# A two-layer decoder trunk on one core: splits of the gated outputs and output weights moved earlier, final norm issued in four pieces

## The chip, the cores and the metric

The kernel runs on one core of a Trainium2 chip, in one launch. The metric is device time in microseconds (us); 1124.77 us is the median of three runs of the kernel before. The engines named below are PE (TensorE, the matmuls), DVE (VectorE), ACT (ScalarE), POOL (GpSimd) and SP (SyncE, which here only issues transfers). Each engine works through its own queue strictly in order, so an instruction that waits holds up everything queued behind it.

## The reference, cut to what matters

Width and sequence length are both 1024, float32 throughout, batch 1, two layers.

```python
# layer 0: gated short convolution;  layer 1: causal differential attention
def diff_attn_mixer(h, w_in, w_out, ...):          # 8 heads, two softmax maps each, V_DIM = 128
    q, k, v, z = jnp.split(h @ w_in, 4, axis=-1)
    ...
    a = p[:, :, 0] - lam * p[:, :, 1]              # difference of two softmaxes
    o = einsum(a, v)                               # per head
    o = rmsnorm(o, subln_g) * (1.0 - lambda_init)  # per-head norm
    return (o * jax.nn.silu(z)) @ w_out            # the gated output y = o * silu(z), then w_out

for i in range(2):
    x = x + mixer_i(rmsnorm(x, norm_g[i]))
return rmsnorm(x, final_g)                         # the final norm
```

## The kernel before

Everything is held transposed: features on the 128 partitions, tokens along the free axis. A 1024 x 1024 operand is eight tiles of 128 features by 1024 tokens. A matmul in full precision is made of three cheaper ones: each operand is split into a high part (rounded to the matmul's format) and a low part (what is left), and `mm3` (line 132) sums high x high, high x low and low x high. So before any operand can be multiplied it must be split: one copy that rounds (`xh`, `wh` or `wo`) and one subtraction (`xl`, `wl`, or the second `wo`). For eight feature tiles and 512 tokens one output takes 24 matmuls.

The attention layer runs as 64 rounds, `step(s)`, head by head and 128 queries at a time, in an order written out by hand; nothing is rescheduled. In each round PE computes scores, DVE finds their maximum, ACT the exponentials, DVE, ACT and POOL the difference of the two maps, and SP issues a transposing transfer of it, which the values product reads three to four rounds later. From round 56 on `opening` and `closing` add work for the output product: weights of the last layer are fetched (`fetch_w`), scaled by the sub-norm's gain and split (`prep_w`: two ACT passes, lines 884 and 885, one subtraction, line 886), and the gated outputs of the heads, stored to memory earlier, are fetched two heads at a time (`fetch_y`) and split (`splits`, `split_y`: ACT line 855, DVE line 856). In the names of the trace these splits are `xh` and `xl` once more, read from `yr`, because they take over the tiles of the layer's input.

After round 63 `tail` computes the outputs of the first 512 tokens. Outputs 0, 2 and 3 are built up as heads become ready, then 1 and 4, then 5, 6 and 7. Head 7 comes last: `last_factors` and the function `rest` it returns spread its norm factors over the partitions with two matmuls (`bps`, line 955), multiply (line 956) and split. `out_take` (a take, line 903) adds the residual on DVE, and has ACT square and scale the sum (lines 910, 915) and POOL add up the squares (line 912). Then come the second 512 tokens in two blocks of 256, eight outputs each, 24 matmuls per output.

`finish` is the final norm of a block, a generator: `next(ending)` issues its next piece. Its pieces are given out between the outputs of the next block: DVE sums up and splits the squares, PE adds them over the partitions (`cps`), POOL takes the root, DVE spreads the result to `dg`, PE broadcasts it (`bps`, line 188), and POOL multiplies and SP stores pair by pair.

Buffers that matter here: the accumulators `mm` are three, used in turn, so an output can start only when the take three outputs earlier has been done; fetched `yr` and `wr` tiles share three slots; the residuals `xr` have two slots each for even and odd outputs.

Of the kernel before, what the change touches and what calls it, by code (L numbers as in the profile page):

```python
# [11 lines left out]
F32 = mybir.dt.float32  # L12
F32R = mybir.dt.float32r
# [4 lines left out]
ALU = mybir.AluOpType  # L18
# [32 lines left out]
def trunk(ctx: ExitStack, tc: tile.TileContext, a: dict, out: bass.AP):  # L51
# [4 lines left out]
    def f(t):  # L56
        return t.bitcast(F32)
# [103 lines left out]
    def norm_cols(sqs, n, rdst, tmp=None):  # L161

        if tmp:
            for sq in sqs[1:]:
                V.tensor_tensor(out=sqs[0], in0=sqs[0], in1=sq, op=ALU.add)
            sqs = bf16_parts(sqs[0], *tmp, (V, V))
        cps = col_sums(sqs, n)
        ms = const.tile([P, KC], F32, tag="ms", bufs=1, name="ms")
        V.tensor_scalar(out=ms[:, :n], in0=cps, scalar1=1.0 / D, scalar2=EPS, op0=ALU.mult, op1=ALU.add)
        G.tensor_tensor(out=rdst, in0=ms[:, :n], in1=neghalf[:, :n], op=ALU.pow)  # L170
# [20 lines left out]
    def norm_rows(rsrc, dst, n, tags, at=None):  # L191

        for b0 in range(0, n, 4):
            nb = min(4, n - b0)
            dgs = sl.tile([P, 2, nb, P], F32R, tag=tags[b0 // 4 % len(tags)], name="dg")
            dgs = dgs[:, 0], dgs[:, 1]
            spread(rsrc[:, b0:b0 + nb], dgs, V)
            bps = rows(dgs, nb, at or ((psm, "mm") if b0 else None))
            if dst is not None:
                A.activation(out=dst[:, b0 * P:(b0 + nb) * P], in_=bps, func=AF.Copy)  # L200
        return bps
# [648 lines left out]

    yh, yl = [], []

    def split_y(h, half, yr):
        s = HALF[half]
        A.activation(out=yh[h][:, s], in_=yr, func=AF.Copy)  # L855
        V.tensor_tensor(out=yl[h][:, s], in0=yr, in1=f(yh[h])[:, s], op=ALU.subtract)  # L856

    raw_y = {}

    def fetch_y(h, half):  # L860

        raw_y[h, half] = yr = r_raw[0].tile([P, 2, 512], F32, name="yr")
        for i in range(2):
            dma(out=yr[:, i, :], in_=yd[h + i, half])

    def splits(h, half):
        yr = raw_y.pop((h, half))
        for i in range(2):
            split_y(h + i, half, yr[:, i, :])

    raw_w = {}

    def fetch_w(d):
        raw_w[d] = r_raw[0].tile([P, D], F32, name="wr")
        dma(out=raw_w[d], in_=a["w_out1"][d])

    def prep_w(d, eng=V):

        wr = raw_w.pop(d)
        if d < 2:  # L880
            wh, wl = (wp.tile([P, D], F32R, tag=t, bufs=2, name=t) for t in ("wh", "wl"))
        else:
            wh, wl = (sl.tile([P, D], F32R, tag=t, name="wo") for t in wtags[d])
        A.activation(out=wr, in_=wr, func=AF.Copy, scale=gsub)
        A.activation(out=wh, in_=wr, func=AF.Copy)
        eng.tensor_tensor(out=wl, in0=wr, in1=f(wh), op=ALU.subtract)
        wo[d] = wh, wl
# [29 lines left out]
    def finish(t0, n, x3s, accs):  # L917

        nb = n // P
        end = t0 + n == S  # L920
        rc = const.tile([P, 4], F32, tag="rc", bufs=2, name="rc")
        tmp = None if end else (sm.tile([P, n], F32, tag="dgl", name="r1"), sm.tile([P, n], BF16, tag="sqw", name="r2"))
        norm_cols(accs, nb, rc[:, :nb], tmp)
        yield
        rt = None if end else r_bc[:, t0:t0 + n]
        rps = norm_rows(rc, rt, nb, r_z.tags[1:])
        yield
        eng, r = (V, rps[:, :n]) if end else (G, rt)
        for d in range(0, KC, 2):
            pair = x3s[d // 2]  # L930
            eng.tensor_tensor(out=pair, in0=pair, in1=r.unsqueeze(1).to_broadcast([P, 2, n]), op=ALU.mult)
            if not end:
                yield
            dma(out=out[d:d + 2, :, t0:t0 + n].rearrange("d p t -> p d t"), in_=pair)
        yield
# [41 lines left out]
    def opening(s):  # L977

        if s == 56:
            q0, q1, q2, q3, spare = (r_q.tags[(r_q.n + 3 + i) % 5] for i in range(5))  # L980
            r_raw.append(Ring(sl, [spare, (wp, "wr0"), (wp, "wr1")]))
            wtags.update({2: r_v.tags[:2], 3: (q0, q1), 5: (q2, q3), 6: r_k.tags[2:]})
            fetch_w(2)
        elif s == 59:
            fetch_w(3)
            fetch_w(0)
        elif s == 61:
            fetch_y(0, 0)
            fetch_y(2, 0)
        elif s == 62:  # L990
            fetch_w(1)
        elif s == 63:
            fetch_y(4, 0)

    def closing(s):

        if s == 56:
            pb = [r_p2.tags[(r_p2.n + i) % 3] for i in (1, 2, 0)]
            wtags.update({4: (r_k.tags[1], pb[0]), 7: (pb[1], pb[2])})
        elif s == 57:  # L1000
            prep_w(2, G)
        elif s == 60:
            prep_w(3, G)
            prep_w(0, G)
        elif s == 61:
            yh[:], yl[:] = new_x()
        elif s == 62:
            splits(0, 0)
        elif s == 63:
            splits(2, 0)  # L1010
            differences(L7, 7)
            for fn in turns:
                fn()
            turns.clear()
            for d in (0, 2, 3):
                pts[d] = psm.tile([P, 512], F32, tag="mm", name="mm")
                part(pts[d], d, 0, 512, (0, 1))
            for t0, n in ((0, 512), (512, 256), (768, 256)):
                order = (0, 2, 3, 1, 4, 5, 6, 7) if not t0 else range(KC)
                wanted.extend((d, t0, n) for d in order)  # L1020

    def tail():
        for d in (0, 2, 3):
            part(pts[d], d, 0, 512, (2, 3))
        head_sums(*last_squares)
        gate_last(0)
        step(NS, False)
        rest = last_factors(0, r_p1.tags[4])
        splits(4, 0)
        split_y(L7 - 1, 0, heads[L7 - 1]["o"][:, HALF[0]])  # L1030
        prep_w(1)
        fetch_w(4)
        fetch_w(5)
        for i in range(3):
            fetch_residual(*wanted.pop(0))
        for d in (0, 2, 3):
            part(pts[d], d, 0, 512, (4, 5, 6))
        pts[1] = pss.tile([P, 512], F32, tag="sc", name="big")
        part(pts[1], 1, 0, 512, range(7))
        step(NS + 1, False)  # L1040
        rest(psa.tile([P, 512], F32, tag="av", name="bps"))
        prep_w(4)
        prep_w(5)
        fetch_w(6)
        fetch_w(7)
        pts[4] = pss.tile([P, 512], F32, tag="sc", name="big")
        part(pts[4], 4, 0, 512, range(7))
        step(NS + 2, False)
        step(NS + 3, False)
        x3a = x3_tiles([r_p1.tags[4], r_p1.tags[0], r_p1.tags[1], r_z.tags[0]], 512)  # L1050
        accs = []
        for d in (0, 2, 3, 1, 4):
            part(pts[d], d, 0, 512, (7,))
            out_take(d, pts[d], 0, 512, x3a, accs)
        fetch_y(0, 1)
        prep_w(6)
        prep_w(7)
        fetch_y(2, 1)
        fetch_y(4, 1)
        pts[5] = psm.tile([P, 512], F32, tag="mm", name="mm")  # L1060
        part(pts[5], 5, 0, 512, range(KC))
        head_sums(*last_squares)
        step(NS + 4, False)
        gate_last(1)
        rest = last_factors(1, r_v.tags[2])
        split_y(L7 - 1, 1, heads[L7 - 1]["o"][:, HALF[1]])
        out_take(5, pts[5], 0, 512, x3a, accs)
        splits(0, 1)
        pt = psm.tile([P, 512], F32, tag="mm", name="mm")
        part(pt, 6, 0, 512, range(KC))  # L1070
        rest(psa.tile([P, 512], F32, tag="av", name="bps"))
        out_take(6, pt, 0, 512, x3a, accs)
        splits(2, 1)
        splits(4, 1)
        pt = psm.tile([P, 512], F32, tag="mm", name="mm")
        part(pt, 7, 0, 512, range(KC))
        out_take(7, pt, 0, 512, x3a, accs)
        ending = finish(0, 512, x3a, accs)
        for t0, tags in ((512, r_v.tags[2:]), (768, r_p1.tags[2:4])):
            x3b = x3_tiles(tags, 256)  # L1080
            accs = []
            for d in range(KC):
                pt = psm.tile([P, 512], F32, tag="mm", name="mm")
                part(pt[:, :256], d, t0, 256, range(KC))
                out_take(d, pt[:, :256], t0, 256, x3b, accs)
                if d:
                    next(ending, None)
            ending = finish(t0, 256, x3b, accs)
        for _ in ending:
            pass  # L1090

# [55 lines left out]
```

## Time and profile before

| what | value |
|---|---|
| median of three runs (lowest, highest) | 1124.77 us (1123.16, 1127.71) |
| the profiled execution, its own time | 1124.44 us |
| its span, first to last instruction | 1122.7 us |
| PE busy | 1062.3 us (95% of the span) |
| DVE, ACT, POOL busy | 595.9, 438.1, 529.9 us |
| mean granted PE clock | 0.967 of full speed |

The profile is of one execution. Its span is 1.7 us shorter than its own device time. All stamps below are microseconds from the start of the span. In a timeline row the first number is the start, the second the time of the merged group, `x3` how many were merged, and the bracket how long the engine stood idle just before and what released it. Busy time of PE is modelled, and a busy PE may still run at half clock.

### The profile page before, as it was taken

Reading aid. Unit: us, or ns where it says so; the run is one execution under the profiler, and the core shown is the slowest. Engines: PE = TensorE matmul, PEld = TensorE weight load, DVE = VectorE, ACT = ScalarE, POOL = GpSimd, SP = SyncE. Lnnn points to the kernel's source line nnn. Section 1 sums busy time; section 2 is a strip of 40 time slices with the busy share of each in tenths; the row PEclk is TensorE's granted clock in tenths of the full one; section 3 lists DMA queues with packets and bytes.
Section 4 is the critical chain, followed back from the end, with each engine's and each line's share of the span. In section 5 each row is a group of like instructions: output and inputs, shape, how many; then the busy total and the mean of one; then the engine's idle time right before and its main releaser. Section 6 shows DMA issues by size and latency. Waiting matters only on the chain.

```text
span 1122.7 us, 15168 instructions
## 1 busy us (share of the span) xinstructions
PE 1062.3 (95%) x5900; PEld 901.2 (80%) x5900; DVE 595.9 (53%) x948; ACT 438.1 (39%) x715; POOL 529.9 (47%) x318
## 2 busy tenths in 40 slices
PE   9899999999999999979979999999999999878896
PEld 6678888888888888868868989888898988656696
DVE  6564133232233322347868686877787687843512
ACT  3211011111111233145746466564656464635322
POOL 7554244244333254345535657383756646412243
PEclk9899999999999999988989999999999999898988
DMA  6221111111111243143474949595656778452132
GB/s 188 76 76 38 57 51 44 57 38 57 40 55 57 100 169 121 67 104 99 101 117 91 173 86 170 95 131 128 140 126 141 132 117 155 108 133 103 51 109 85
DMA packets 123192, 111.86 MB, mean 100 GB/s; under 512 B 88128, under 2 KB 95984, under 8 KB 123120
## 3 DMA queue, kind: packets, MB, share of 16 engines
q1 hardware_dynamic: 123120, 110.90, 42.3%
q8 instruction: 46, 0.75, 0.3%
q14 instruction: 26, 0.21, 0.1%
HBM read 67.82 MB, written 11.59 MB: 71 GB/s over the span
## 4 chain that ended last, share of the span: by engine, by line
PE 77%; DVE 7%; DMA 5%; POOL 5%; ACT 3%; issue 2%; SPq 0%; POOLq 0%; DVEq 0%; ACTq 0%
PE big L132 37%; PE mm L132 25%; PE sc L616 5%; PE mm L525 5%; DMA p<-p 3%; PE av L672 3%; DVE p L639 1%; PE cps L157 1%; POOL p L652 1%; POOL wl L408 1%; DVE nm L621 1%; POOL qt L465 1%; DMA xr<-in_xT 1%; ACT p L644 1%; POOL w3l L254 0%
## 5 line engine op out<-in xcount | busy, mean ns | idle before, releaser
L120 POOL TENSOR_TENSOR wl<-wr,wh 128x1024 fp32r<-128x1024 f32 x37 | 90.1, 2435 | 215.9 <-ACT wh L119 215.9
L132 PE MATMUL mm<-xh,wh 128*128 128x512 f32 (+1 forms) x424 | 163.3, 385 | 4.2 <-ACT xh L855 4.1
L132 PE MATMUL mm<-xl,wh 128*128 128x512 f32 (+1 forms) x424 | 163.8, 386 | 2.9 <-DVE xl L856 2.9
L132 PE MATMUL mm<-xh,wl 128*128 128x512 f32 (+1 forms) x424 | 162.6, 384 | 0.0
L119 ACT ACTIVATE wh<-wr 128x1024 fp32r<-128x1024 f32 x37 | 39.2, 1061 | 294.4 <-PE big L132 293.6
L132 PE MATMUL big<-xh,wh 128*128 128x512 f32 x472 | 146.9, 391 | 2.2 <-DVE cr L289 2.2
L132 PE MATMUL big<-xh,wl 128*128 128x512 f32 x472 | 146.8, 391 | 0.0
L132 PE MATMUL big<-xl,wh 128*128 128x512 f32 x472 | 146.7, 390 | 0.0
L408 POOL TENSOR_TENSOR wl<-wr,wh 128x1024 fp32r<-128x1024 f32 x40 | 95.9, 2398 | 104.2 <-ACT wh L407 99.8
L623 ACT ACTIVATE p<-sc,nm 128x256 f32<-128x256 f32 (+7 forms) x128 | 94.2, 739 | 44.9 <-DVE nm L621 20.8
L132 PEld LDWEIGHTS big<-xh,wh 128*128 128x128 f32 x472 | 88.8, 189 | 20.9 <-issue 2.6
L132 PEld LDWEIGHTS big<-xh,wl 128*128 128x128 f32 x472 | 89.1, 189 | 18.5
L132 PEld LDWEIGHTS big<-xl,wh 128*128 128x128 f32 x472 | 88.9, 188 | 18.6
L132 PEld LDWEIGHTS mm<-xh,wh 128*128 128x128 f32 x424 | 80.2, 189 | 19.9 <-ACT xh L855 5.6
L132 PEld LDWEIGHTS mm<-xl,wh 128*128 128x128 f32 x424 | 80.2, 189 | 18.8 <-DVE xl L856 4.7
L621 DVE TENSOR_REDUCE nm<-sc 128x2 f32<-128x256 f32 (+5 forms) x96 | 91.9, 958 | 3.3
L132 PEld LDWEIGHTS mm<-xh,wl 128*128 128x128 f32 x424 | 80.3, 189 | 15.6
L616 PE MATMUL sc<-kt,qt 128*128 128x512 f32 (+2 forms) x384 | 86.2, 360 | 4.7 <-issue 2.0
L525 PE MATMUL mm<-wh,xh 128*128 128x256 f32 x256 | 74.9, 293 | 1.3 <-DVE tq L460 0.6
L616 PEld LDWEIGHTS sc<-kt,qt 128*128 128x128 f32 x384 | 64.4, 193 | 13.0 <-ACT p L623 3.2
L525 PE MATMUL mm<-wl,xh 128*128 128x256 f32 x256 | 74.5, 291 | 0.0
L525 PE MATMUL mm<-wh,xl 128*128 128x256 f32 x256 | 74.4, 290 | 0.0
(190 smaller groups left out, 2016.5 us busy)
## 6 DMA issues: line engine op xcount, KB each, us to landing
wr<-in_w_in SPq DMA_DIRECT2D x53, 512.0 KB, 3.5
wr<-in_w_out SPq DMA_DIRECT2D x16, 512.0 KB, 4.4
wr<-in_w_v SPq DMA_DIRECT2D x16, 512.0 KB, 3.8
qt<-qt SPq DMA_DIRECT2D x32, 256.0 KB, 3.9
xr<-in_xT SPq DMA_DIRECT2D x15, 512.0 KB, 4.3
x2d<-x SPq DMA_DIRECT2D x8, 512.0 KB, 2.8
kt<-lo SPq DMA_DIRECT2D x32, 128.0 KB, 4.8
rb<-rrd SPq DMA_DIRECT2D x14, 256.0 KB, 4.8
```

The source lines that it names most:

```text
L119: A.activation(out=wh, in_=wr, func=AF.Copy)
L120: G.tensor_tensor(out=wl, in0=wr, in1=f(wh), op=ALU.subtract)
L132: T.matmul(ps[:, o:o + n], lhsT=w[:, s], rhs=r[k][:, t:t + n], start=(k == 0 and r is rh and w is wh), stop=(k == KC - 1 and w is wl))
L157: T.matmul(cps[:, b:b + 1], lhsT=part[:, b * P:(b + 1) * P], rhs=one, start=(i == 0), stop=(i == len(parts) - 1))
L408: G.tensor_tensor(out=self.wl, in0=self.wr, in1=f(self.wh), op=ALU.subtract)
L465: G.tensor_tensor(out=qt[own[m], 1, :], in0=tq[own[m]], in1=f(qt)[own[m], 0, :], op=ALU.subtract)
L525: T.matmul(self.pts[tp][:, i, :], lhsT=x[k][:, ts], rhs=w[:, kk], start=(k == 0 and i == 0 and x is xh and w is wh), stop=(k == KC - 1 and ...
L616: T.matmul(sc[:, i, c0:c1_], lhsT=qt[:, var, ts], rhs=kt[:, c0:c1_], start=(var == 0), stop=(var == 1))
L621: V.tensor_reduce(out=nm[:, ms], in_=sc[:, :, :L], axis=AX, op=ALU.max, negate=True)
L623: A.activation(out=(p1_, p2_)[m][:, :L], in_=sc[:, i, :L], func=AF.Exp, bias=nm[:, m:m + 1], accum_out=st[:, m:m + 1])
L639: V.scalar_tensor_tensor(out=p1_[:, :L], in0=p2_[:, :L], scalar=cs[:, 1:2], in1=p1_[:, :L], op0=ALU.mult, op1=ALU.add)
L672: T.matmul(av[:, qi * P:(qi + 1) * P], lhsT=v[:, kb, es], rhs=at[:, r, :], start=(kb == 0 and r == 0 and v is vh), stop=(kb == qb and v is ...
```

## The change

The diff, whole. `V`, `A`, `G` are DVE, ACT and POOL.

```diff
-    def split_y(h, half, yr):
+    def split_y(h, half, yr, pool=0):
+
         s = HALF[half]
-        A.activation(out=yh[h][:, s], in_=yr, func=AF.Copy)
-        V.tensor_tensor(out=yl[h][:, s], in0=yr, in1=f(yh[h])[:, s], op=ALU.subtract)
+        if pool == 2:
+            G.tensor_copy(out=yh[h][:, s], in_=yr)
+        else:
+            A.activation(out=yh[h][:, s], in_=yr, func=AF.Copy)
+        (G if pool else V).tensor_tensor(out=yl[h][:, s], in0=yr, in1=f(yh[h])[:, s], op=ALU.subtract)
...
-    def splits(h, half):
+    def splits(h, half, pool=(0, 0)):
         yr = raw_y.pop((h, half))
         for i in range(2):
-            split_y(h + i, half, yr[:, i, :])
+            split_y(h + i, half, yr[:, i, :], pool[i])
...
-        tmp = None if end else (sm.tile([P, n], F32, tag="dgl", name="r1"), sm.tile([P, n], BF16, tag="sqw", name="r2"))
-        norm_cols(accs, nb, rc[:, :nb], tmp)
+        if not end:
+            V.tensor_tensor(out=accs[0], in0=accs[0], in1=accs[1], op=ALU.add)
+            accs = bf16_parts(accs[0], sm.tile([P, n], F32, tag="dgl", name="r1"),
+                              sm.tile([P, n], BF16, tag="sqw", name="r2"), (V, V))
+            yield
+        norm_cols(accs, nb, rc[:, :nb])
         yield
         rt = None if end else r_bc[:, t0:t0 + n]
-        rps = norm_rows(rc, rt, nb, r_z.tags[1:])
+        dgs = sl.tile([P, 2, nb, P], F32R, tag=r_z.tags[1], name="dg")
+        dgs = dgs[:, 0], dgs[:, 1]
+        spread(rc[:, :nb], dgs, V)
+        yield
+        rps = rows(dgs, nb)
+        if not end:
+            A.activation(out=rt, in_=rps, func=AF.Copy)
         yield
...
@@ opening
         elif s == 62:
             fetch_w(1)
+            splits(0, 0, (1, 2))
         elif s == 63:
             fetch_y(4, 0)
+            split_y(2, 0, raw_y[2, 0][:, 0, :], 2)
@@ closing
-        elif s == 62:
-            splits(0, 0)
         elif s == 63:
-            splits(2, 0)
+            split_y(3, 0, raw_y.pop((2, 0))[:, 1, :])
@@ tail
         step(NS + 1, False)
+        prep_w(4)
         rest(psa.tile([P, 512], F32, tag="av", name="bps"))
-        prep_w(4)
         prep_w(5)
...
         accs = []
+        prep_w(6)
         for d in (0, 2, 3, 1, 4):
             part(pts[d], d, 0, 512, (7,))
             out_take(d, pts[d], 0, 512, x3a, accs)
+            if d == 3:
+                prep_w(7)
         fetch_y(0, 1)
-        prep_w(6)
-        prep_w(7)
...
         part(pt, 6, 0, 512, range(KC))
-        rest(psa.tile([P, 512], F32, tag="av", name="bps"))
+        splits(2, 1, (2, 0))
         out_take(6, pt, 0, 512, x3a, accs)
-        splits(2, 1)
-        splits(4, 1)
+        splits(4, 1, (0, 2))
         pt = psm.tile([P, 512], F32, tag="mm", name="mm")
         part(pt, 7, 0, 512, range(KC))
+        rest(psa.tile([P, 512], F32, tag="av", name="bps"))
         out_take(7, pt, 0, 512, x3a, accs)
         ending = finish(0, 512, x3a, accs)
+        next(ending)
...
                 if d:
                     next(ending, None)
+            for _ in ending:
+                pass
             ending = finish(t0, 256, x3b, accs)
+            next(ending)
```

The first place is POOL's queue at rounds 61 to 64. `xh` and `xl` are the splits of the gated outputs (of heads 0, 1 and 2 here), `o` the gating of head 6, `p` the low halves of the attention differences of head 7. Before:

```order
L494 TENSOR_TENSOR o<-o,rb 128x512
L494 TENSOR_TENSOR o<-o,th 128x512
L494 TENSOR_TENSOR o<-o,rb 128x512
L494 TENSOR_TENSOR o<-o,th 128x512
L652 TENSOR_TENSOR p_8277<-p_8276,p_8277 128x768
L652 TENSOR_TENSOR p_8358<-p_8357,p_8358 128x896
```

And now:

```order
L494 TENSOR_TENSOR o<-o,rb 128x512
L494 TENSOR_TENSOR o<-o,th 128x512
L860 TENSOR_TENSOR xl_8342<-yr,xh_8334 128x512
L857 CAST xh_8335<-yr 128x512
L860 TENSOR_TENSOR xl_8343<-yr,xh_8335 128x512
L494 TENSOR_TENSOR o<-o,rb 128x512
L494 TENSOR_TENSOR o<-o,th 128x512
L857 CAST xh_8336<-yr 128x512
L860 TENSOR_TENSOR xl_8344<-yr,xh_8336 128x512
L652 TENSOR_TENSOR p_8277<-p_8276,p_8277 128x768
L652 TENSOR_TENSOR p_8362<-p_8361,p_8362 128x896
```

Two rounding copies and three subtractions have come onto POOL, two of the five ahead of the difference's halves; the first rounding copy stays on ACT, a round earlier than it was.

The second place is DVE's queue where the first outputs are taken: `x<-mm,xr` and `x<-big,xr` are the takes of outputs 0, 2, 3 and then 1, 4; `wo<-wr,wo` the last step of splitting a weight. Before:

```order
L886 TENSOR_TENSOR wo<-wr,wo 128x1024 x2
L676 TENSOR_SCALAR o<-av,us 128x256
L903 TENSOR_TENSOR x_8714<-mm,xr 128x512
L903 TENSOR_TENSOR x_8715<-mm,xr 128x512 x2
L903 TENSOR_TENSOR x_8714<-big,xr 128x512
L903 TENSOR_TENSOR x_8716<-big,xr 128x512
L886 TENSOR_TENSOR wo<-wr,wo 128x1024 x2
```

And now:

```order
L890 TENSOR_TENSOR wo<-wr,wo 128x1024
L676 TENSOR_SCALAR o<-av,us 128x256
L890 TENSOR_TENSOR wo<-wr,wo 128x1024
L907 TENSOR_TENSOR x_8714<-mm,xr 128x512
L907 TENSOR_TENSOR x_8715<-mm,xr 128x512 x2
L890 TENSOR_TENSOR wo<-wr,wo 128x1024
L907 TENSOR_TENSOR x_8714<-big,xr 128x512
L907 TENSOR_TENSOR x_8716<-big,xr 128x512
```

The weight of output 6 now stands ahead of the first take, that of output 7 between the takes of outputs 3 and 1.

The third place is DVE's queue at the end of the first 512 tokens. `x<-mm,xr 128x512` is the take of output 7, the ones of 128x256 those of the next block; L165 (now L927), L147 and L148 sum and split the squares. Before:

```order
L903 TENSOR_TENSOR x_8717<-mm,xr 128x512
L903 TENSOR_TENSOR x_8916<-mm,xr 128x256 x2
L165 TENSOR_TENSOR acc<-acc,sq 128x512
L147 TENSOR_TENSOR r_8982<-acc 128x512
L148 TENSOR_TENSOR r_8983<-r_8982 128x512
L169 TENSOR_SCALAR ms<-cps 128x4
L903 TENSOR_TENSOR x_8916<-mm,xr 128x256
```

And now:

```order
L907 TENSOR_TENSOR x_8717<-mm,xr 128x512
L927 TENSOR_TENSOR acc<-acc,sq 128x512
L147 TENSOR_TENSOR r_8918<-acc 128x512
L148 TENSOR_TENSOR r_8919<-r_8918 128x512
L907 TENSOR_TENSOR x_8922<-mm,xr 128x256 x2
L169 TENSOR_SCALAR ms<-cps 128x4
L907 TENSOR_TENSOR x_8922<-mm,xr 128x256
```

The three instructions that sum and split the squares have moved ahead of the takes of the next block's first two outputs.

## Rows read from the trace of the kernel before

**Rows 1.** Waits of PE, 940 to 1123 us; in total, times, longest, us

```profile
PE bps L188 <- DVE dg L180: 5.1, 4, 1.9
```

**Rows 2.** Timeline of PE, start of the splits of heads 2 and 3

```profile
984.55 0.49 PE L132 MATMUL mm<-xh,wh 128*128 128x512 f32 x1 [3.23 <-ACT xh L855]
986.54 0.79 PE L132 MATMUL mm<-xl,wh 128*128 128x512 f32 x1 [1.49 <-DVE xl L856]
```

**Rows 3.** Timeline of DVE, rounds 62 to 64

```profile
974.62 1.29 DVE L856 TENSOR_TENSOR xl<-yr,xh 128x512 fp32r<-128x512 f32 x2 [1.79 <-ACT xh L855]
...
979.92 2.00 DVE L639 SCALAR_TENSOR_TENSOR p<-p,cs,p 128x896 f32<-128x896 f32 x1
984.53 2.56 DVE L856 TENSOR_TENSOR xl<-yr,xh 128x512 fp32r<-128x512 f32 x2 [2.61 <-ACT xh L855]
...
987.51 1.28 DVE L639 SCALAR_TENSOR_TENSOR p<-p,cs,p 128x1024 f32<-128x1024 f32 x1
```

**Rows 4.** Timeline of POOL, the same rounds

```profile
976.72 1.28 POOL L494 TENSOR_TENSOR o<-o,rb 128x512 f32<-128x512 f32 x1 [8.04 <-DVE sc L619]
...
979.32 1.66 POOL L652 TENSOR_TENSOR p<-p,p 128x768 f16<-128x768 f32 x1
984.06 1.88 POOL L652 TENSOR_TENSOR p<-p,p 128x896 f16<-128x896 f32 x1 [3.08 <-ACT p L645]
```

**Rows 5.** Timeline of PE, outputs 4 to 7 and the second half's first

```profile
1011.49 0.80 PE L132 MATMUL big<-xh,wo 128*128 128x512 f32 x1 [3.57 <-ACT wo L885]
...
1019.05 2.69 PE L672 MATMUL av<-p,vt 128*128 128x128 f16 x45
...
1025.08 0.39 PE L132 MATMUL mm<-xh,wo 128*128 128x512 f32 x1
...
1030.53 0.95 PE L157 MATMUL cps<-ones_r,sqo 128*128 128x1 f32 x8
1034.35 0.80 PE L132 MATMUL mm<-xh,wo 128*128 128x512 f32 x1 [2.87 <-ACT wo L885]
...
1043.10 0.64 PE L955 MATMUL bps<-dg,ones_r 128*128 128x512 f32 x2
...
1049.07 0.28 PE L132 MATMUL mm<-xh,wh 128*128 128x256 f32 x1
```

**Rows 6.** Windows: length, busy us of each engine, granted clock, DMA share

```profile
1007.90:1019.05 11.15, 7.54 (x22) 5.34 (x21) 3.83 (x4) 4.82 (x5) 0.00 (x0) 0.69 0.21 71
...
1031.48:1043.10 11.62, 8.72 (x24) 6.46 (x25) 5.92 (x10) 6.28 (x8) 2.86 (x3) 0.71 0.29 102
```

**Rows 7.** Groups by line and shape, 1005 to 1055 us

```profile
L912 POOL TENSOR_TENSOR acc<-acc,sq 128x512 f32<-128x512 f32 x6 | 7.8, 1293 | 41.6 <-ACT sq L910 41.6
...
L886 DVE TENSOR_TENSOR wo<-wr,wo 128x1024 fp32r<-128x1024 f32 x4 | 4.9, 1226 | 10.8 <-ACT wo L885 10.8
L884 ACT ACTIVATE wr<-wr,gsub 128x1024 f32<-128x1024 f32 x4 | 4.5, 1134 | 0.0
L910 ACT ACTIVATE sq<-x 128x512 f32<-128x512 f32 x7 | 4.4, 629 | 10.3 <-DVE x L903 8.3 <-POOL acc L912 2.0
L885 ACT ACTIVATE wo<-wr 128x1024 fp32r<-128x1024 f32 x4 | 4.2, 1056 | 0.1
```

**Rows 8.** Timeline of DVE, takes of the second half's blocks

```profile
1053.86 0.42 DVE L903 TENSOR_TENSOR x<-mm,xr 128x256 f32<-128x256 f32 x1 [0.71 <-PE mm L132]
...
1080.52 0.42 DVE L903 TENSOR_TENSOR x<-mm,xr 128x256 f32<-128x256 f32 x1 [2.46 <-PE mm L132]
1083.40 0.42 DVE L903 TENSOR_TENSOR x<-mm,xr 128x256 f32<-128x256 f32 x1 [2.46 <-PE mm L132]
...
1111.88 0.42 DVE L903 TENSOR_TENSOR x<-mm,xr 128x256 f32<-128x256 f32 x1 [2.46 <-PE mm L132]
```

**Rows 9.** Groups by line and shape, POOL, the whole span

```profile
L379 POOL TENSOR_TENSOR acc<-acc,sq 128x1024 f32<-128x1024 f32 x6 | 18.0, 2999 | 2.0 <-ACT sq L377 2.0
...
L298 POOL TENSOR_SCALAR t<-v,cw 128x1024 f32<-128x1024 f32 x8 | 9.4, 1180 | 0.0
```

## The prediction, on record before the changed kernel ran

> **What bounds the kernel now.** PE is busy for 95% of the span, so time can only come from the places where it stands idle or runs at half clock. I read the waits of PE over the last 180 us first, then its timeline there, then the timelines of the engines that it waited for. The reader is to see three kinds of place. PE waits for gated outputs to be split: 3.23 us and, two us later, 1.49 us [rows 2]. It waits for the weights of outputs 4 and 6: 3.57 and 2.87 us [rows 5]. And it waits for the final norm, of which the spread tiles alone cost 5.1 us in four waits [rows 1]. A wait costs more than its length: after the two weight waits PE ran at the lower of its two clock levels (1.2 GHz) for several us, the windows around them having a granted clock of 0.69 and 0.71 [rows 6]. At the full level 24 matmuls of 512 columns take 1030.53 - 1025.08 = 5.45 us, 0.227 each [rows 5].
>
> **The change, term by term.** Times are of the profiled execution; a minus is a gain.
>
> *1. First splits, a round earlier.* Before, two subtractions (1.29 us) and 1.79 us of waiting for ACT stood on DVE ahead of round 63: 3.1 us that go, and everything behind on DVE and ACT starts that much earlier [rows 3]. Against it, POOL now does five operations there. It stood idle for 8.04 us before the gating at 976.72 [rows 4], so the first three are covered (subtraction 1.28 twice, and the rounding copy). The second copy and subtraction, some 2 us, stand in front of the low halves of the differences; their transposed product is read by PE well behind, and POOL waits for ACT again before the last of them, so this costs nothing on its own. But DVE's steps now run beside POOL. The difference of 896 columns took 2.00 us beside POOL's 1.66 us operation, while one of 1024 columns with POOL idle took 1.28; and the second pair of subtractions took 2.56 us beside POOL's 1.88 instead of 1.29 [rows 3, 4]. The earlier gating puts one such collision (up to 1.28 us) onto the difference of 896 columns, and one subtraction instead of two gives 0.6 back, with up to 1.3 of collision. That is -3.1 + 1.2 - 0.6 to -1.9: I take **-3.0**, between -1.5 (another POOL operation of 1.66 us in the way) and -5.0 (no new collision).
>
> *2. Weight of output 4 ahead of head 7's last split.* Before, ACT reached it only after PE had broadcast head 7's factors. Now ACT does it some 6 us before PE needs it; its transfer has landed by then, since its slot is released by the split of head 3, which is not later. The wait of 3.57 goes, and with it the half clock: 1019.05 - 1011.49 = 7.56 us for 21 matmuls that take 4.77 at full rate [rows 5]. 3.57 + 2.79 = **-6.4**. Head 7's split is behind it, but is needed only at the last step of each output.
>
> *3. New wait at output 5.* The weight of output 6 now stands on DVE ahead of the first take. From the end of the values product: eviction 0.4, ACT's square 0.63, its two weight passes 1.13 and 1.06, DVE's subtraction 1.23, the take 0.69, hand-offs 0.2: 5.3 us, the four in the middle by [rows 7]. PE has 15 matmuls in that time, 3.4 us, and then needs the accumulator that the first take frees: 1.9 us of waiting. After it the clock may fall: nothing to 3.3 us (row of the longer wait); I take 1.4. **+3.3**, between +1.9 and +5.2.
>
> *4. Weight of output 6 ready.* Gone are 2.87 us and the half clock of output 6, 1043.10 - 1034.35 - 5.45 = 3.30 [rows 5]: **-6.2**. That of output 7 is ready by my count some 8 us before its turn. The takes of outputs 1 and 4 come later behind it, and with them the transfers of the second half's gated outputs, queued on SP behind the residual of output 7, which needs the slot of output 1's take. By the same count they still land about 5 us before ACT wants them.
>
> *5. Second half's splits.* Before, its first output took from 1049.07 to 1053.86 [rows 5, 8], 1.7 us over the 2.88 of an undisturbed one (1083.40 - 1080.52, [rows 8]), 0.2 of it the hand-off. PE now arrives sooner, but ACT, DVE and POOL do not: take, square, scale, sum and splits are a chain through all three. From the first split that starts the output, DVE has two more subtractions (1.2) and the take of output 6 (0.69), ACT its square (0.63), POOL the sum (1.29), a rounding copy and a subtraction (1.28) [rows 4, 7]; then the last third of the output, 1.1. The rounding copy is in no row. POOL's one-input operation on twice the elements took 1.18 us, so 0.6 is the lower bound; its slowest two-input one on twice the elements took 3.0, the upper [rows 9]. I take 0.7, near the one-input row. Sum 6.9, with hand-offs and collisions 7.6: 4.8 over. Head 7's factors now come after output 7's matmuls, and end within this. **+3.1**, between +2 and +6.
>
> The Trainium skill, GPSIMD Engine Reference, section 3.1, gives 769 ns measured for 512 elements in a tight loop; a copy at that price would move the sum by under 0.3 us.
>
> *6. Norm of the first 512 tokens.* From the take at 1053.86 to that at 1083.40 are 29.54 us for seven outputs, 20.16 at 2.88: 9.38 too much [rows 8]. Now the sum and splits run on DVE while PE does two outputs (5.8 us), the spreading while it does a third. The norm's own matmuls (0.9) and about 0.5 of waiting stay: **-8.0**, between -6.0 and -8.4. The multiplications and stores come one output later; the residuals queued behind the stores on SP are fetched three outputs ahead, which covers it.
>
> *7. Norm of the first 256.* 1111.88 - 1083.40 = 28.48 for eight, 23.04 at 2.88: 5.44 over [rows 8], of which 0.6 stay: **-4.8**, between -4.0 and -5.0. The tail behind 1111.88 has the same instructions as before. POOL's last pair now comes behind the last sum, but ends before the root is wanted.
>
> Sum: -3.0 - 6.4 + 3.3 - 6.2 + 3.1 - 8.0 - 4.8 = **-22.0**. The profiled execution took 1124.44, so 1102.4; the median of the runs is 0.33 above that execution, and I say **1102.5 us**. The ends together give 1124.4 - 27.4 = 1097 and 1124.4 - 13 = 1111.
>
> **Rivals.**
>
> *A. POOL and DVE stand in each other's way throughout.* For it: the 2.00 and 2.56 us above. Against: takes and evictions read an accumulator, and the half of the tail where DVE is nearly idle has time to lose. Price: term 1 at nothing, term 5 at +6, terms 6 and 7 at -6.5 and -4.4: -14.2, **1110 us**. Beside it: the Trainium skill, SBUF — State Buffer, "Who interferes with whom", says that GpSimd and a VectorE instruction with two SBUF inputs exclude each other, and that the first holds the port pair for its whole instruction. By that rule the work put onto POOL is not free for DVE even where POOL is idle; the trace agrees: 896 columns took 2.00 us beside a POOL operation, 1024 columns alone 1.28.
>
> *B. The final norm in four pieces does not hide.* Its root on POOL is queued behind the sum of the next block's second output, and DVE's spread behind the take of the third; if these arrive after PE has finished the following output, terms 6 and 7 vanish: 1124.4 - 9.2 = **1115 us**. Against: by my count the spread is ready about 1 us early.
>
> *C. The rounding copy on POOL is slow (the slower side).* No row shows this form. Its place is POOL's queue, four times. With e us above 0.7 each, the first hides in the idle 8 us up to e = 4.8, the second has 2 us of room, the other two stand on PE's path: 4e - 6.8. At e = 7.2 all 22 us are gone; at e = 8.6 (a copy of 9.3 us) the kernel is 5.6 us slower, **1130 us**. Against: nothing of POOL's on this size comes near.
>
> **How the numbers follow.** My forecast with its own spread (1097 to 1107) has 0.70, A 0.15, B 0.07, C 0.08, half of it within 0.5% and half slower; 0.5%, 5.6 us, is about what a measurement of this kernel can tell from no change. Faster: 0.70 + 0.15 + 0.07 = 0.92; same 0.04; slower 0.04. The range 1097 to 1111 holds the forecast and A and leaves out B and C.
>
> **What would show it.** In the new profile PE should not wait for `wo` before outputs 4 and 6, but some 2 us for the take ahead of output 5; the second half's first output should take about 7.5 us; the takes of the second half should be 2.9 to 3.4 us apart throughout; the rounding copy on POOL should take under 1 us. I am wrong if DVE's subtractions and differences beside POOL stretch to 2 us each and more (A), if the spread tiles still show up among PE's waits (B), or if the copy exceeds 3 us (C).

## The result and the profile after

The changed kernel took **1108.44 us** (median of 4 runs, 1104.69 to 1109.88), the kernel before 1123.97 on the same chip (four runs, the three above and one more): a ratio of 0.9845, 95% interval 0.9822 to 0.9868. The forecast was 1102.5, with a range of 1097 to 1111: faster as foretold, but 15.5 us of gain instead of 22. The profiled execution has a span of 1107.9 us (before 1122.7), and in it the last take comes 14.60 us earlier.

I compare the profiled runs by instructions that both have, and sum a term from one such milestone to the next. "Net" means that the run's start is taken off, by the scores that PE begins at 959.01 us before and at 959.28 after. The first view is of what PE waits for over the whole span after: engine, line, for whom; us in total, times, the longest.

```profile
PE sc L616 <- ACT p L623: 5.2, 1, 5.2
PE mm L132 <- DVE xl L860: 4.9, 5, 1.5
PE mm L132 <- ACT xh L859: 4.0, 3, 1.6
PE bps L188 <- DVE dg L180: 1.9, 1, 1.9
PE mm L132 <- DVE x L907: 1.8, 1, 1.8
```

No weight `wo` is waited for any more, and of the 5.1 us for the spread tiles of the norm [rows 1] one wait of 1.9 is left. The waits for split outputs (`xl`, `xh`) are not shorter, though: 8.9 us in all, first and second half together, where before they were 7.0. And a wait of 5.2 us for ACT's exponentials is new.

PE's timeline after (start, duration, engine, line, operation; in brackets the idle time before, and what ended it), at the places of [rows 2] and [rows 5], with DVE's takes of the second half under it, for [rows 8]:

```profile
985.12 0.49 PE L132 MATMUL mm<-xh,wh 128*128 128x512 f32 x1 [1.45 <-ACT xh L859]
987.11 0.80 PE L132 MATMUL mm<-xl,wh 128*128 128x512 f32 x1 [1.49 <-DVE xl L860]
997.75 0.50 PE L132 MATMUL mm<-xl,wh 128*128 128x512 f32 x1 [1.00 <-DVE xl L860]
1013.88 2.69 PE L672 MATMUL av<-p,vt 128*128 128x128 f16 x45
1021.89 0.47 PE L132 MATMUL mm<-xh,wo 128*128 128x512 f32 x1 [1.82 <-DVE x L907]
1027.46 0.95 PE L157 MATMUL cps<-ones_r,sqo 128*128 128x1 f32 x8
1039.29 0.63 PE L969 MATMUL bps<-dg,ones_r 128*128 128x512 f32 x2
```

```profile
1055.66 0.42 DVE L907 TENSOR_TENSOR x<-mm,xr 128x256 f32<-128x256 f32 x1 [1.84 <-PE mm L132]
1073.78 0.42 DVE L907 TENSOR_TENSOR x<-mm,xr 128x256 f32<-128x256 f32 x1 [2.46 <-PE mm L132]
1097.28 0.42 DVE L907 TENSOR_TENSOR x<-mm,xr 128x256 f32<-128x256 f32 x1 [2.46 <-PE mm L132]
```

The matmul at 997.75 and the take at 1055.66 (the second half's second output) stood here before:

```profile
996.50 0.50 PE L132 MATMUL mm<-xl,wh 128*128 128x512 f32 x1 [1.08 <-DVE xl L856]
1056.73 0.42 DVE L903 TENSOR_TENSOR x<-mm,xr 128x256 f32<-128x256 f32 x1 [2.45 <-PE mm L132]
```

The other two takes stood at 1083.40 (the first 256 tokens' last) and 1111.88. The second half starts when PE is free for it: after, at 1039.77, behind the two matmuls of 1039.29, which take 0.48 us. From that:

| term | from, to (after) | forecast | measured |
|---|---|---|---|
| 1 first splits | start, 997.75 | -3.0 | +1.25, net +1.0 |
| 2 weight 4 | 997.75, 1013.88 | -6.4 | -6.4 |
| 3 wait at output 5 | 1013.88, 1027.46 | +3.3 | +2.1 |
| 4 weight 6 | 1027.46, second half's start at 1039.77 | -6.2 | -6.2 |
| 5 second half's splits | 1039.77, 1055.66 | +3.1 | +8.2 |
| 6 norm, first 512 | 1055.66, 1073.78 | -8.0 | -8.6 |
| 7 norm, first 256 | 1073.78, 1097.28 | -4.8 | -5.0 |
| sum | | -22.0 | net -14.9 |

Term 5 runs here to the second take, while the forecast's ended with the first output. That output took 11.3 us where it had taken 4.6, and the second another 1.5 more than before; with the boundary of the forecast term 5 is +6.7 and term 6 -7.0.

Each milestone is read from one profile, and can be off by about 1 us with the same instructions up to there. Net of its start, that of term 1 lies at 37.5, 38.5 and 38.7 us in the three kernels that have the old splits (the kernel before and two of the experiments below), and at 36.0 to 38.5 in the four that have the new splits with the late fetch. By the means term 1 is -0.7 us: no loss, but far from -3.0.

Two terms hold the miss: the first by 4.0 us, the fifth by 5.1. ACT's timeline shows the place of the first, and the row of the chain of waits under it what ACT waited for (start, us, what):

```profile
965.13 0.83 ACT L647 ACTIVATE p<-p,cs 128x640 f16<-128x640 f32 x1 [0.73 <-DVE p L639]
972.21 0.63 ACT L859 ACTIVATE xh<-yr 128x512 fp32r<-128x512 f32 x1 [6.24 <-DMA yr<-yd]
```

```profile
960.19 11.93 DMA yr<-yd
```

The first rounding copy, now a round ahead, came to ACT before its data: the fetch took 12 us to land. It is no slower than before (11.5 to 12.8 us there for the same four), but then ACT got to it only at 974. Round 62's exponentials stand behind it, and PE's scores behind those.

For term 5 the view is PE in the second half's first output, then DVE and POOL beside it, then the row of the windows for the stretch (us; busy us and instructions of PE, PEld, DVE, ACT, POOL; granted clock; DMA share; GB/s):

```profile
1040.82 0.38 PE L132 MATMUL mm<-xh,wh 128*128 128x256 f32 x1 [0.89 <-ACT xh L859]
1042.00 0.38 PE L132 MATMUL mm<-xl,wh 128*128 128x256 f32 x1 [0.79 <-DVE xl L860]
1043.68 0.39 PE L132 MATMUL mm<-xl,wh 128*128 128x256 f32 x1 [1.06 <-DVE xl L860]
1046.87 0.58 PE L132 MATMUL mm<-xh,wh 128*128 128x256 f32 x1 [1.63 <-ACT xh L859]
1048.04 0.58 PE L132 MATMUL mm<-xl,wh 128*128 128x256 f32 x1 [0.59 <-DVE xl L860]
1051.05 0.41 PE L132 MATMUL mm<-xh,wh 128*128 128x256 f32 x1
```

```profile
1038.08 0.68 DVE L907 TENSOR_TENSOR x<-mm,xr 128x512 f32<-128x512 f32 x1
1040.80 3.42 DVE L860 TENSOR_TENSOR xl<-yr,xh 128x512 fp32r<-128x512 f32 x3 [2.03 <-ACT xh L859]
```

```profile
1040.79 0.61 POOL L857 CAST xh<-yr 128x512 fp32r<-128x512 f32 x1
1041.48 1.60 POOL L860 TENSOR_TENSOR xl<-yr,xh 128x512 fp32r<-128x512 f32 x1
1047.52 1.60 POOL L860 TENSOR_TENSOR xl<-yr,xh 128x512 fp32r<-128x512 f32 x1
```

```profile
1040.00:1056.00 16.00, 10.98 (x62) 9.66 (x63) 9.81 (x14) 6.59 (x12) 6.41 (x6) 0.68 0.10 32
```

The first output took from 1039.77 to 1051.05, 11.3 us where the forecast was 7.6, and the second 4.4 where an undisturbed one takes 2.9: from 1044.40 to 1054.5 PE ran at 1.2 GHz (0.21 us from matmul to matmul instead of 0.12). Three subtractions on DVE took 3.42 us beside POOL's 1.60; I had reckoned 1.8.

### The profile page after: what moved, and what is told of

Its sections match the earlier page's. It is cut to its first block, busy times and chain, and to the rows that moved or that the text cites. A ratio compares the mean times of both kernels' runs of the same rounds, so it can differ in the third digit from the quotient of the medians.

```text
span 1107.9 us, 15173 instructions
## 1 busy us (share of the span) xinstructions
PE 1053.9 (95%) x5900; PEld 896.9 (81%) x5900; DVE 598.5 (54%) x943; ACT 435.4 (39%) x711; POOL 540.8 (49%) x327
## 4 chain that ended last, share of the span: by engine, by line
PE 75%; DMA 7%; DVE 6%; POOL 6%; ACT 3%; issue 2%; SPq 0%; POOLq 0%; DVEq 0%; ACTq 0%
PE big L132 37%; PE mm L132 23%; PE sc L616 5%; PE mm L525 5%; DMA p<-p 4%; PE av L672 3%; DVE p L639 1%; POOL wl L408 1%; PE cps L157 1%; DMA yr<-yd 1%; POOL p L652 1%; DVE nm L621 1%; POOL qt L465 1%; POOL acc L916 1%; DMA xr<-in_xT 1%
```

## The experiments

Ratios are to the kernel before on the same chip, with 95% intervals.

**The fetch of heads 0 and 1 two rounds earlier**

```diff
         elif s == 59:
             fetch_w(3)
             fetch_w(0)
+            fetch_y(0, 0)
         elif s == 61:
-            fetch_y(0, 0)
             fetch_y(2, 0)
```

> The changed kernel, with the transfer of the gated outputs of heads 0 and 1 issued at round 59 instead of 61. Theory 'late transfer': in the changed kernel ACT waited 6.2 us for that transfer (12 us from issue to landing) and round 62's exponentials stood behind it, which cost term 1 its 3.0 us and 1.25 more. Then ACT should not wait for it now, PE's wait before round 63's scores should fall from 5.2 to about 1.7 us, and the kernel should be 3 to 5 us faster than the changed one (about 1104). Rival 'port': POOL's new work beside DVE takes the gain in these rounds anyway; then the wait goes but the first subtraction for head 4 comes no more than 1.5 us earlier, and the time stays within 1.5 us of the changed kernel (1107 to 1109).

1102.06 us, ratio 0.9816 (0.9792 to 0.9839): below the changed kernel by 3 us by the ratios and 6 by the medians. ACT's copy and the matmul that ends term 1:

```profile
964.49 0.62 ACT L859 ACTIVATE xh<-yr 128x512 fp32r<-128x512 f32 x1
992.21 0.50 PE L132 MATMUL mm<-xl,wh 128*128 128x512 f32 x1 [1.64 <-DVE xl L860]
```

The fetch landed in 5.2 us, ACT's copy started at 964.49 instead of 972.21, and PE's wait for the exponentials fell to 1.7 us, as before. The matmul at 997.75 came at 992.21; net of the start (957.89) that is 3.2 us earlier than in the kernel before, the -3.0 of term 1. What failed in that term was the transfer.

**The weight of output 7 behind the takes**

```diff
         for d in (0, 2, 3, 1, 4):
             part(pts[d], d, 0, 512, (7,))
             out_take(d, pts[d], 0, 512, x3a, accs)
-            if d == 3:
-                prep_w(7)
         fetch_y(0, 1)
+        prep_w(7)
```

> The changed kernel, with the weight of output 7 split behind the takes of outputs 1 and 4 instead of ahead of them. Theory 'queue': those two takes waited from about 1020 to 1029.8 for that weight, and with them the squares, POOL's sums, head 6's root behind the sums, the take of output 5, and so the splits of the second half, which kept PE waiting five times and at half clock. Then the takes of outputs 1 and 4 should follow the others at once, the second half's first two outputs should take 6 to 8 us together instead of about 15.7, and the kernel should be 5 to 8 us faster than the changed one (about 1102). Rival 'POOL splits': the two heads split on POOL and their collisions with DVE are what holds the second half up; then this gains under 2 us.

1107.30 us, ratio 0.9857 (0.9833 to 0.9881): no difference to the changed kernel that can be told. DVE's timeline:

```profile
1024.96 0.69 DVE L907 TENSOR_TENSOR x<-big,xr 128x512 f32<-128x512 f32 x1 [1.11 <-DMA xr<-x2d]
1033.01 1.23 DVE L890 TENSOR_TENSOR wo<-wr,wo 128x1024 fp32r<-128x1024 f32 x1 [7.36 <-ACT wo L889]
1034.15 0.22 DVE L690 TENSOR_SCALAR rr<-cps,ec 128x4 f32<-128x4 f32 x1
1037.97 0.68 DVE L907 TENSOR_TENSOR x<-mm,xr 128x512 f32<-128x512 f32 x1
```

The takes of outputs 1 and 4 followed at once, but DVE then stood idle for 7.36 us in front of the weight, with the scaling of the sum (`rr`) behind it and the take of output 5 behind that, at 1037.97 as good as at 1038.08. The wait had only moved down the queue.

**The second half's splits not on POOL**

```diff
-        splits(2, 1, (2, 0))
+        splits(2, 1)
...
-        splits(4, 1, (0, 2))
+        splits(4, 1)
```

> The changed kernel, with all splits of the second half on ACT and DVE again (at their new places), none on POOL. Rival 'POOL splits': 3 to 5 us faster than the changed kernel (about 1104). Theory 'queue': the chain starts as late as before, DVE and ACT have two more splits each; within 1.5 us of the changed kernel, rather slower (1108 to 1110).

1106.73 us, ratio 0.9856 (0.9831 to 0.9882): by the times no difference that can be told. In the trace the way from the sum matmul after output 5 to the second half's second take is 1052.32 - 1026.70 = 25.62 us where the changed kernel has 28.20. Four subtractions now took less than three did:

```profile
1038.42 2.50 DVE L860 TENSOR_TENSOR xl<-yr,xh 128x512 fp32r<-128x512 f32 x4 [2.04 <-ACT xh L859]
```

So some 2.6 us of the 5.1 that term 5 missed hang on POOL's part, the collisions and what the clock did behind them together.

**The early fetch, weight 6 a step earlier, weight 7 late**

Beside the early fetch of heads 0 and 1; weight 7 leaves its place between the takes:

```diff
+        prep_w(6)
         step(NS + 2, False)
...
-        prep_w(6)
...
         fetch_y(0, 1)
+        prep_w(7)
```

> The changed kernel with both: heads 0 and 1 fetched at round 59, weight 7 behind the takes; and the weight of output 6 split before head 7's last values product, so that it does not stand ahead of the first take. If 'late transfer' and 'queue' both hold they add up, and the wait of 1.8 us ahead of output 5 goes too: 9 to 13 us faster than the changed kernel (1096 to 1100). If the waits only move on to the transfers of the second half's gated outputs, which are queued behind the residuals: 5 to 8 us (1100 to 1104).

1099.90 us, ratio 0.9795 (0.977 to 0.982). The wait ahead of output 5 (term 3) is gone, and the sum matmul after output 5 follows the values product in 11.47 us (1020.88 - 1009.41) instead of 13.58: -2.1, the whole of the term.

**The norm, the weights and the splits, each alone on the kernel before**

The change's three parts. The norm alone is the edit of `finish` with the added calls of `next(ending)`; the weights alone are `prep_w(4)` ahead of `rest`, and `prep_w(6)` and `prep_w(7)` at their new places; the splits alone are the rest of the diff.

> The kernel before with only the final norm cut into four pieces between the units (terms 6 and 7 of the prediction); splits and weights stand where they stood. Theory: the milestones gave -8.55 us for the first 512 tokens and -4.98 for the first 256, and both pieces lie behind everything else that was changed, so alone they give -13.5 us: some 1110.5 us where the kernel before has 1124. The waits of PE for the spread tiles (5.1 us before) fall to about 2. Rival B: without the earlier weights and splits the sums of the second half come late, the norm waits again in other places, and less than half of it, under 7 us, is left: over 1117 us.

1112.15 us, ratio 0.9883 (0.9849 to 0.9917): -13.1 us by the ratio. Of PE's waits for the spread tiles 1.9 us are left (`PE bps L188 <- DVE dg L180: 1.9, 1, 1.9`). The norm hides whether or not the rest comes earlier; rival B falls.

> The kernel before with only the weights of outputs 4, 6 and 7 prepared earlier (terms 2 to 4). Up to the start of the second half this should be worth -6.4 + 2.1 - 6.2 = -10.5 us by the milestones. Theory of the lost term 5: the first output of the second half hangs on a chain of takes, squares, sums and splits that does not move with PE, so most of that is given back there: 5 to 8 us, and the kernel gains 2 to 5 us (1119 to 1122). Rival (the splits on POOL are what made the second half's first output long): with the splits still on ACT and DVE nothing is given back, and the kernel gains 8 to 10 us (1114 to 1116).

1119.87 us, ratio 0.9961 (0.994 to 0.9982): -4.4 us. The second half's start moved by 5.9 us (1049.07 to 1043.20), its second take by only 3.1 (1056.73 to 1053.67). The take of output 6 (1047.33 to 1043.79) and the splits behind it came 3.5 us earlier, PE 5.9, and so the first output was long also with no split on POOL, with a wait of 2.46 us for ACT and then half clock:

```profile
1046.52 0.51 PE L132 MATMUL mm<-xh,wh 128*128 128x256 f32 x1 [2.46 <-ACT xh L855]
```

The time fell into the range expected, but not by the sum expected: 10.5 us up to the second half's start, of which 5 to 8 are given back, were 5.9 and 2.8. Of the missing 4.6, 1.6 are half clock behind the wait ahead of output 5, which the changed kernel did not have in its profile (see the fetch ahead of the element store, below), and 1.7 a wait for head 7's spread tiles, since `rest` stands in its old place here.

> The kernel before with only the splits changed (terms 1 and 5 of the prediction): first splits a round ahead, a part of them and of the second half's on POOL, head 7's factors of the second half behind output 7. Theory: the milestones of the changed kernel gave +1.25 us for the first splits, since they wait for a transfer that lands 12 us after its issue, and the run with the second half's splits off POOL was 2.6 us shorter there, so alone they gain nothing: 0 to +4 us, 1123.5 to 1127.5. Together with the norm alone (-13.1 by its ratio) and the weights alone (-4.4) this should come near the -17.4 of the whole change. Rival (the splits do gain 3 us as term 1 said, and only the weights spoil it): 1120 to 1121.

1125.02 us, ratio 1.0008 (0.9988 to 1.0027): +0.9 us. In this kernel, too, PE waits for the exponentials behind the late transfer, and of the two waits of [rows 2] only the first shrinks, to 1.27 us; the second stays at 1.48:

```profile
PE sc L616 <- ACT p L623: 5.8, 1, 5.8
```

-13.1 - 4.4 + 0.9 = -16.6 us, near the -17.4 that the ratio of the whole change gives: within their intervals the parts add up, and the headline part, splitting a round ahead and partly on POOL, gave nothing.

**The fetch just ahead of the element store**

```diff
         if last:
             last.third()
+        if s == 60:
+            fetch_y(0, 0)
         store_factors()
...
-            fetch_y(0, 0)
```

> The changed kernel with one swap on SP: the fetch of heads 0 and 1 is issued just ahead of the store of 512 single elements of round 60 (and by that at the end of that round), no longer just behind it. Theory (a transfer queued behind that store lands late): the fetch lands in 4 to 6 us, by 966 instead of 972, ACT does not wait for it (6.2 us before), and the kernel gains the 5 to 6 us that the fetch two rounds earlier gave: 1102 to 1103.5. Rival (it is slow because of everything else that moves in this stretch): it still takes 10 to 12 us to land, at 970 or so, ACT waits some 4 us, and the gain is under 2.5 us: 1106 to 1108.

1104.39 us, ratio 0.9825 (0.98 to 0.985). SP's queue after (start, us, issues), and the landing times of that fetch:

```profile
959.62 0.53 SPq L701 DMA_DIRECT2D rrd<-rr  x1
960.19 2.68 SPq L868 DMA_DIRECT2D yr<-yd  x4
```

```profile
DMA to landing us min/median/max: 11.4/12.0/12.8
```

The same two views of this kernel, the second for the pair ahead of the store alone:

```profile
958.07 1.07 SPq L870 DMA_DIRECT2D yr<-yd  x2
959.24 0.38 SPq L701 DMA_DIRECT2D rrd<-rr  x1
960.59 0.81 SPq L870 DMA_DIRECT2D yr<-yd  x2
```

```profile
DMA to landing us min/median/max: 3.1/3.1/3.1
```

Heads 0 and 1 land in 3.1 us; heads 2 and 3, still behind the store, in 9.5 to 13.1. ACT's wait is gone. The gain is 4 us by the medians and 2 by the ratios, under the 5 to 6 expected. At 979.83 PE now waits 3.73 us for the copy that POOL makes, but that is not where the gain went: the matmul that ends term 1 comes 34.6 us behind the start, with the fetch two rounds earlier 34.3. In the profile 1.6 us are lost later, at output 5:

```profile
1016.54 0.47 PE L132 MATMUL mm<-xh,wo 128*128 128x512 f32 x1 [1.82 <-DVE x L909]
1023.68 0.95 PE L157 MATMUL cps<-ones_r,sqo 128*128 128x1 f32 x8
```

The wait is the 1.82 us of the changed kernel, but the output takes 7.14 us instead of 5.57, at a granted clock of 0.76 instead of 1.00. The same wait left the clock at 1.00 with the fetch two rounds earlier and with weight 7 behind the takes, and was followed by 0.76 in the runs with no second-half split on POOL and with the weights alone. What decides it is not shown.

**Weight 7 in the factors' wait**

Beside the early fetch and the early weight 6 (weight 7 leaves its place between the takes):

```diff
         gate_last(1)
+        prep_w(7)
         rest = last_factors(1, r_v.tags[2])
```

> Beside the earlier fetch of heads 0 and 1 and the earlier weight of output 6 (1099.9 us), the weight of output 7 is prepared behind the gating of the second half's last head, where DVE waits for the root on POOL, no longer ahead of the sum's scaling. Theory (the weight on DVE ahead of the factors holds the chain that starts the second half): the scaling comes at 1021.9 instead of 1025.7, the take of output 5 some 1.8 us earlier than 1029.5, and the second half's second take 1.8 to 2.5 us earlier: 1097.5 to 1098 us. Rival (the chain is bound by ACT's squares and POOL's sums, which take 2.03 us for each output): the take of output 5 stays at 1029 or so and the time within 0.7 us of 1099.9.

1096.61 us, ratio 0.9759 (0.9727 to 0.979). DVE's scaling of the sum and take of output 5, first with weight 7 ahead of them (the run of 1099.90 us), then behind:

```profile
1024.55 1.23 DVE L890 TENSOR_TENSOR wo<-wr,wo 128x1024 fp32r<-128x1024 f32 x1 [7.39 <-ACT wo L889]
1025.69 0.22 DVE L690 TENSOR_SCALAR rr<-cps,ec 128x4 f32<-128x4 f32 x1
1029.51 0.69 DVE L907 TENSOR_TENSOR x<-mm,xr 128x512 f32<-128x512 f32 x1
```

```profile
1018.08 0.22 DVE L690 TENSOR_SCALAR rr<-cps,ec 128x4 f32<-128x4 f32 x1 [4.72 <-PE cps L157]
1020.78 1.23 DVE L890 TENSOR_TENSOR wo<-wr,wo 128x1024 fp32r<-128x1024 f32 x1 [1.01 <-ACT wo L889]
1024.00 0.68 DVE L907 TENSOR_TENSOR x<-mm,xr 128x512 f32<-128x512 f32 x1
```

From the sum matmul (1020.88 and 1017.09) to the scaling it is 4.8 us in the one and 1.0 in the other, to the take 8.6 and 6.9; the second half's second take follows the sum matmul after 23.7 us instead of 25.9. The weight on DVE did hold the chain that starts the second half.

**The take of output 5 ahead of the factors**

```diff
         part(pts[5], 5, 0, 512, range(KC))
+        out_take(5, pts[5], 0, 512, x3a, accs)
...
-        out_take(5, pts[5], 0, 512, x3a, accs)
```

> The same, and the take of output 5 is written ahead of the second half's factors on DVE: PE has finished that output 8.6 us before DVE takes it in the run with 1099.9 us. Theory (order on DVE): the take comes at about 1021.5, its square, sum and scaling are done before the factors, the first splits of the second half start at 1028 instead of 1031.6, the take of output 6 comes at 1032 instead of 1035.5, and PE's waits in the second half's first output (3.5 us, with some 2 us at half clock) shrink to about 1: 3 to 5 us less, 1095 to 1097. Rival (the root on POOL, now queued behind one more sum of 1.3 us, puts the factors as late as the take was before): under 1 us, 1098 to 1099.

1095.75 us, ratio 0.9741 (0.9711 to 0.9772): no difference to the run before it that can be told, and 3 to 5 us had been expected.

```profile
1023.36 0.69 DVE L907 TENSOR_TENSOR x<-mm,xr 128x512 f32<-128x512 f32 x1 [3.89 <-PE mm L132]
1024.15 0.22 DVE L690 TENSOR_SCALAR rr<-cps,ec 128x4 f32<-128x4 f32 x1
1028.88 1.22 DVE L890 TENSOR_TENSOR wo<-wr,wo 128x1024 fp32r<-128x1024 f32 x1 [3.04 <-ACT wo L889]
```

The take came at once, but weight 7 came 2.0 us later behind its square on ACT (sum matmul to weight: 5.7 us instead of 3.7), and the factors behind that. PE's waits in the second half's first output fell from 3.1 to 1.7 us, and the way from the sum matmul to the second take by 1.1. The same run was 1.4 us later already at the sum matmul, net of its start, where nothing was edited.

Both of these last versions beat the changed kernel, by 10 and 12 us by the ratios.

## Why the prediction was partly right

**Right:** the direction, the bound (waits of PE and the half clock behind them), and five of seven terms within 1.2 us. The weights' waits of [rows 5] went with their half clock; the norm hides behind the following outputs; the rounding copy takes 0.61 or 0.62 us in three of its four places and 1.07 in one, near the 0.7 chosen, and C falls. Term 3 cost 2.1 of 3.3: its wait was 1.82 us as counted, but the clock held; from 1021.89 to 1039.77 PE was granted 1.00. That was luck: in three experiments the same wait was followed by half clock, and the term was +3.7. That the time stayed inside the range is luck in part too: terms 1 and 5 left their own ranges on the slow side, by 2.5 and 2.2 us, and terms 3 and 6 stayed off their slow ends by 3.1 and 2.6.

**Wrong, term 1.** The failing step is "everything behind on DVE and ACT starts that much earlier". I had counted what left DVE, and found POOL idle; but the first copy moved past round 62's exponentials on ACT, and its transfer, issued at 960.19, landed 12 us later. Before, ACT came too late for that to be seen; the landing times of these four fetches could be read from the trace of before, and I did not read them. With the fetch earlier the term is -3.2, inside its range, and -3.7 by the mean of the five kernels that have it.

**Wrong, term 5.** The mechanism was right (PE arrives sooner than the chain), the size was not: +8.2 instead of +3.1, or +6.7 with the boundary of the forecast, beyond its upper end of 6 either way. Two things are missing from its sum. One is collisions: DVE's three subtractions 3.42 us for 1.8, POOL's 1.60 for 1.28, together 1.9 on the chain; that is rival A's mechanism at this one place, and taking POOL out gave 2.6 us back. The other is the clock, which the term left out altogether: the last third of the first output took 1.9 us for 1.1, and the second 4.4 for 2.9, 2.3 us. By this count the remaining 0.9 are hand-offs and the 0.4 us from PE's arrival to ACT's first copy. I had put the price of a clock that falls onto term 3, where PE waited once; it fell at 1044.40, where PE had waited three times, and stayed down over two more waits. No run takes the clock's part away by itself; it is read from the rows alone.

Two figures of the working are off by a little: the lower ends of the terms add up to 27.1 and not 27.4, and 7.6 is 4.7 over 2.88 and not 4.8. Neither moves the range or the forecast by more than 0.3 us.

A as a whole falls, though its 1110 us is nearer to the time than the forecast is: terms 6 and 7 show nothing of it, and what term 1 lost came from the transfer. DVE did stretch beside POOL's multiplications there, with one subtraction of 128x256 at 2.51 us (1075.71) where the same one in the kernel before took 0.42; but DVE had the time to lose. The Trainium skill, SBUF — State Buffer, "Who interferes with whom", lets whichever of GpSimd and VectorE starts first hold the shared port pair for its whole instruction; by that rule, the 2.51 us are a wait for POOL's multiplication, and the trace agrees as far as that: each of those takes 2.40 to 2.48 us, and the one in question ends at 1077.94, 0.28 us ahead of the subtraction's end.

## What to carry to other kernels

Work that is moved a round ahead moves past its data too: read from the trace when each of its inputs lands, the ones hidden until now above all. Taking waits from one engine buys only what the chain of the other engines leaves; follow that chain to the first instruction that stands in order behind something foreign to it (here a weight ahead of a sum's scaling, 2.2 us in the trace), and price a falling clock wherever an engine will wait several times in a row. Before a term of 1 us is believed, see how far the same milestone moves between profiles of kernels that do not differ there.

## What the runs showed of the hardware

- A store of 512 single elements (2 KB), that of round 60, took 9.5 to 9.9 us to land in the five kernels where it was read by itself, and fetches of 256 KB issued just behind it on the same queue 9.5 to 13.3 us, in all twelve. The same fetch ahead of the store landed in 3.1 us, and two rounds earlier in 5.2. That the position behind the store decides is shown by the swap; whether it is the queue's order or the shared transfer engines was not tried.
- Three subtractions of 128x512 on DVE took 3.42 us beside one of POOL's, four without 2.50; POOL's own took 1.60 instead of 1.28.
- Behind one and the same wait of 1.82 us ahead of output 5 the granted clock over that output was 1.00 in three kernels and 0.76 in three others (1.6 us longer). In the second half's first output PE went to 1.2 GHz at 1044.40, right behind three waits of 0.79 to 1.06 us, and kept to it until 1054.5, the last 6 us of that with no wait longer than 0.4.
